# Where the second mixer's first weight pieces are loaded and converted, relative to the last down-projection stage

## The chip, the cores and the metric

The kernel runs on one core of one Trainium2 chip. The metric is the device time of one execution in microseconds (us), lower is better. Three timed executions of the kernel before took 2145.69, 2148.03 and 2148.07 us; their median, 2148.03 us, is its time. A fourth execution was taken with the hardware profiler; all rows below come from it.

## What is computed

Two residual layers of a transformer-like trunk, in float32, over 256 tokens of width 2048. Layer 0 has the "AB" mixer (neighbourhood attention beside a gated recurrence), layer 1 the "CD" mixer (pooling beside grouped-query attention). Each layer is a mixer, a layer norm, a gated feed-forward block and a second layer norm:

```
for layer in range(DEPTH):          # DEPTH = 2
    y = ab_mixer(x, ...) if layer % 2 == 0 else cd_mixer(x, ...)
    x = layer_norm(DN_ALPHA * x + y, ln_mix_g[layer], ln_mix_b[layer])
    f = swiglu(x, ffn_w_gate[layer], ffn_w_up[layer], ffn_w_down[layer])
    x = layer_norm(DN_ALPHA * x + f, ln_ffn_g[layer], ln_ffn_b[layer])

def cd_mixer(x, w_in, w_out, ...):
    proj = x @ w_in                  # 2048 x 2560, five chunks of 512 columns here
    ...
```

The place of interest is the seam between the layers: the end of layer 0's `swiglu` (its down projection), the layer norm behind it, and the first of the five column chunks of `x @ w_in` in layer 1's mixer.

## The kernel before, in words

**Tiling.** The 256 tokens are two blocks of 128, called token 0 and token 1 here (`tok` in the code). A weight matrix is read in pieces of 128 partitions x 2 x 512 float32 (512 KB). For precision every float32 operand is held as two fp32r halves, high and low, and a product is three matmuls (low x high, high x high, high x low; `mm3`, L407). So a piece goes through four steps: SyncE's queue (SP) issues its DMA into one of four buffers `raw` (L290); ScalarE (ACT) casts it to `whi` (L252); VectorE (DVE) subtracts to get `wlo` (L253); TensorE (PE) multiplies. One piece is twelve matmuls, six for each token. `load_half` does the first three steps and gives `whi` and `wlo` a slot from `rings`, some pools of buffers that are taken in turn.

**Two loop orders.** `mm_chunk` either takes a piece for both tokens and then the next piece, or (`tok_major`) loads all its pieces first, runs all of them for token 0, calls `after(0)`, and then runs all of them for token 1. The second order is used around a layer norm, so that the norm of token 0 can run while PE works on token 1.

**The seam.** The last stage of the feed-forward block (`ffn`) multiplies hidden chunks 9 and 10 with the down weights in two `mm_chunk` calls of eight pieces each: columns 0 and 1 of the output first, then columns 2 and 3 in token-major order. I number these sixteen pieces down 0 to down 15. Results lie in PSUM banks `acc` and `mx`, which ACT has seeded with the residual (L422). In `after(tok)`, DVE takes statistics of the banks (`BN_STATS` on tile `st`, L430), combines them (`BN_AGGR`, L436), adds epsilon (L356); GpSimd (POOL) takes the power for `rstd` (L359); DVE centres four columns (L445, reads the norm's gain `gam`); ACT scales them by `rstd` (L459); DVE adds the norm's bias `bet` (L460). `gam` and `bet` are loaded by two 1 MB DMAs (L497, L498).

**The flips.** A normed token then has to be transposed for the next matmuls: four groups of four transposes on PE (L249, into banks `tr` and `mx`), each evacuated by ACT (`xTh`, L486) and DVE (`xTl`, L487). They wait in the generator `pending`, and `mm_chunk` calls `step()` ahead of a piece from number `first_step` on, so that the flips of token 0 stand among the last matmuls of token 1; what is left is run at the end of the token. The constant `LATER` (7) is that number at two places: the down call for columns 2 and 3, and the first chunk of the CD mixer.

**The mixer's first chunk.** `cd_mixer` runs five chunks of eight pieces `cd_in`. Chunk 0 is token-major; its token 0 part needs only token 0's flips, and token 1's norm and flips run beside it. I call its pieces cd 0 to cd 7 and those of chunk 1 c1-0 to c1-7. Chunk 0's two result banks are evacuated by the function `kv` (`dvh`, `dvl`, squares for a norm, `rx` on L1237) before chunk 1's second token can write into the first of them, since the tag `acc` has three banks.

**What sets the order.** Instructions are put on each engine by a scheduler that simulates a timeline; `tc.high_priority` moves a group ahead, `tc.issue_after(ins)` puts what is issued inside it behind `ins`, and `tc.keep_in_program_order` pins one behind the last. Each engine then runs its own list strictly in order. Before the change the eight pieces of chunk 0 are issued by `cd_mixer`, when `ffn` has been written out; the idle y buffers (`new_yT`, three of them, and `fourth`, `y4h` and `y4l`) are set up for the CD mixer's results just before it.

Of the kernel before, what the change touches and what calls it, by code (L numbers as in the profile page):

```python
# [66 lines left out]
LATER = 7  # L67
# [141 lines left out]
def trunk(ctx: ExitStack, tc: tile.TileContext, a, out):  # L209
# [41 lines left out]
    def split(hi, lo, src):  # L251
        nc.scalar.copy(hi, src)  # L252
        return nc.vector.tensor_tensor(lo, src, hi.bitcast(F32), op=sub).ins  # L253
# [15 lines left out]
    held = [0]  # L269
    last_load = [None]  # L270
# [3 lines left out]
    def load_half(src, between=()):  # L274
        behind = ahead if held[0] > 0 else ()
        held[0] -= 1
        slots = [r for r in rings for _ in range(r[1])]
        pool, bufs = rings[0] if turn[0] < 0 else slots[turn[0] * 3 % len(slots) if len(slots) % 3 else turn[0] % len(slots)]
        turn[0] += 1
        with tc.high_priority(offset=400):  # L280
            raw = wp.tile([P, 2, NCH], F32, tag="raw", name="raw", bufs=4)
            hi = pool.tile([P, 2, NCH], F32R, tag="whi", name="whi", bufs=bufs)
            lo = pool.tile([P, 2, NCH], F32R, tag="wlo", name="wlo", bufs=bufs)
            parts = 1 + len(between)
            n = 2 // parts
            for i in range(parts):
                if i:
                    between[i - 1]()
                s = slice(i * n, (i + 1) * n)
                load = nc.sync.dma_start(raw[:, s, :], src[:, s, :])  # L290
                if first[0]:
                    tc.keep_in_program_order(load)
                last_load[0] = load.ins
                with ExitStack() as order:
                    for ins in behind:
                        order.enter_context(tc.issue_after(ins))
                    split(hi[:, s, :], lo[:, s, :], raw[:, s, :])
        return hi, lo
# [5 lines left out]
    def mm_chunk(halves, lhs, outs, tok_major=False, after=None, before=None, seeded=False, first_step=FIRST_STEP, pinned=0):  # L304

        n = len(halves)
        loaded = []
# [16 lines left out]
        if tok_major:  # L324
            for i, half in enumerate(halves):
                src = half[0]
                if pending and i >= FREE:
                    held[0] = 1
                loaded.append(load_half(src))
            for tok in range(NT):  # L330
# [6 lines left out]
                while pending:  # L337
                    step()
                if after:
                    after(tok)  # L340
# [497 lines left out]
    def ffn(layer, xT, res, mix_pool, close_mix, keep, last):  # L838
# [64 lines left out]
        def after(tok):  # L903
# [8 lines left out]
        mm_chunk(some((2, 3), [(ci, j, j) for j in (2, 3) for ci in range(2)]), yl, ends, tok_major=True, after=after, seeded=True, first_step=LATER)  # L912
        rings.pop()
        stack.close()
        return nxt
# [308 lines left out]
    def cd_mixer(mp, consts, xT, yT):  # L1224
# [102 lines left out]
        for c, (kind, _) in enumerate(cd_plan()):  # L1327
            outs = [acc() for _ in range(NT)]
            mm_chunk([(a["cd_in"][c, n], two(2 * n)) for n in range(8)], lhs, outs, tok_major=(c == 0), first_step=LATER)
            if c == 0:  # L1330
                with tc.issue_after(last_load[0]):
# [40 lines left out]
    def layer_end(i, w, groups, yT, last):  # L1372
# [11 lines left out]
        return ffn(i, xT, res, fp, close, keep, last)  # L1384

    consts = []
    xT = layer_end(0, a["ab_out"], AB_OUT_GROUPS, yT, False)
    yT = [new_yT() for _ in range(3)] + [fourth()]
    with tc.tile_pool(name="cd", bufs=1, reuse_waits="tile") as mp:
        cd_mixer(mp, consts, xT, yT)  # L1390
# [114 lines left out]
```

## Time and profile before

| | us |
|---|---|
| median of three timed runs | 2148.03 (2145.69 to 2148.07) |
| the profiled execution | 2149.07 |
| span of its instructions | 2147.3 |
| time outside the span | 1.77 |
| PE busy / DVE busy / ACT busy in the span | 2127.0 / 1763.1 / 1242.4 |
| longest idle time of PE between 10 and 2130 us | 3.35, before the matmul at 1212.69 |
| mean granted TensorE clock, whole span | 0.998 |
| granted TensorE clock, 1212.70 to 1217.20 | 0.62 |

Times of single instructions are counted from the start of the span. A row of a timeline gives start, duration, engine, line and operation with its tiles, and in brackets how long the engine had been idle and what released it. Matmuls are pipelined: one of 512 columns is shown as 0.39 us long, but the next starts 0.227 us later, so it is the distance of starts that counts. The clock column of a table of stretches is the share of full TensorE speed that was granted.

### The profile page before, as it was taken

The page shows a single profiled execution, that of the slowest core. Times are in us where ns is not written, and L with a number is a line of the kernel's source. Part 1 is how long each engine was busy: PE and PEld are TensorE (multiplying, and loading weights), DVE is VectorE, ACT ScalarE, POOL GpSimd, SP SyncE. Part 2 cuts the span into 40 slices and gives each one's busy share as a digit, 9 for nine tenths or more (in the row PEclk, how much of TensorE's full clock was granted, in tenths as well). Part 3 has the DMA queues.
Part 4 walks back from the last instruction along what each step waited for, and adds up shares of the span by engine and source line. Part 5 has one row for each costly group of instructions (what it writes and reads, how often), then busy time and mean ns, then how long its engine had stood idle before and what let it go on. Part 6 is the DMA issues. An engine that isn't in the chain of part 4 may idle for free.

```text
span 2147.3 us, 27217 instructions
## 1 busy us (share of the span) xinstructions
PE 2127.0 (99%) x9856; PEld 1771.6 (83%) x9856; DVE 1763.1 (82%) x2226; ACT 1242.4 (58%) x1618; POOL 37.5 (2%) x43
## 2 busy tenths in 40 slices
PE   8999999999999999999999999999999999999998
PEld 7888888888888888888888788888888888888886
DVE  6885688666789999999996776676999999999976
ACT  6435534555556666666676564454566666667763
POOL 0001001000000000000000000000000000000000
PEclk9999999999999999999999999999999999999999
DMA  8545545584667777767765563564777767777754
GB/s 294 168 152 185 163 157 172 181 283 144 215 250 266 253 257 257 263 237 251 264 243 191 206 233 125 183 210 157 283 255 256 257 243 248 267 247 257 255 186 176
DMA packets 118614, 477.25 MB, mean 222 GB/s; under 512 B 13904, under 2 KB 16976, under 8 KB 103376
## 3 DMA queue, kind: packets, MB, share of 16 engines
q1 hardware_dynamic: 118480, 475.53, 63.6%
q8 instruction: 77, 1.26, 0.2%
q14 instruction: 57, 0.47, 0.1%
HBM read 473.37 MB, written 2.10 MB: 221 GB/s over the span
## 4 chain that ended last, share of the span: by engine, by line
PE 97%; DVE 1%; DMA 1%; issue 0%; ACT 0%; SPq 0%; DVEq 0%; ACTq 0%
PE un L566 35%; PE acc L407 33%; PE acc L566 20%; PE mx L407 4%; PE mx L1057 1%; PE tr L249 1%; PE un L249 1%; DVE wlo L253 1%; DMA raw<-in_cd_in 1%; DMA raw<-in_down 1%; PE mx L1103 0%; PE mx L1318 0%; ACT whi L252 0%; PE mx L249 0%; DMA raw<-in_ab_in 0%
## 5 line engine op out<-in xcount | busy, mean ns | idle before, releaser
L540 ACT CAST whi<-raw 128x1024 fp32r<-128x1024 f32 x356 | 372.9, 1052 | 226.5 <-PE acc L566 72.0
L253 DVE TENSOR_TENSOR wlo<-raw,whi 128x1024 fp32r<-128x1024 f32 (+1 forms) x297 | 359.6, 1220 | 162.5 <-ACT whi L252 160.2
L544 DVE TENSOR_TENSOR wlo<-raw,whi 128x1024 fp32r<-128x1024 f32 x356 | 430.5, 1219 | 70.3 <-ACT whi L540 65.4
L252 ACT CAST whi<-raw 128x1024 fp32r<-128x1024 f32 (+1 forms) x297 | 309.3, 1049 | 298.5 <-PE acc L407 185.1
L407 PE MATMUL acc<-whi,xTl 128*128 128x512 f32 x736 | 293.3, 398 | 8.8 <-ACT whi L252 5.4
L407 PE MATMUL acc<-whi,xTh 128*128 128x512 f32 x736 | 290.9, 395 | 0.0
L407 PE MATMUL acc<-wlo,xTh 128*128 128x512 f32 x736 | 288.3, 395 | 0.0
L566 PE MATMUL acc<-whi,yTl 128*128 128x512 f32 x576 | 225.8, 392 | 0.0
L566 PE MATMUL acc<-wlo,yTh 128*128 128x512 f32 x576 | 224.4, 390 | 0.0
L566 PE MATMUL acc<-whi,yTh 128*128 128x512 f32 x576 | 224.1, 389 | 0.0
L540 ACT CAST sh<-z 128x1024 fp32r<-128x1024 f32 x108 | 113.6, 1052 | 128.6 <-DVE z L637 73.5
L566 PE MATMUL un<-whi,xTl 128*128 128x512 f32 x460 | 179.0, 389 | 0.0
L566 PE MATMUL un<-whi,xTh 128*128 128x512 f32 x460 | 178.9, 389 | 0.0
L566 PE MATMUL un<-wlo,xTh 128*128 128x512 f32 x460 | 178.9, 389 | 0.0
L407 PEld LDWEIGHTS acc<-whi,xTl 128*128 128x128 f32 x736 | 139.5, 190 | 36.7 <-ACT whi L252 6.1
L407 PEld LDWEIGHTS acc<-wlo,xTh 128*128 128x128 f32 x736 | 139.3, 189 | 28.1 <-DVE wlo L253 0.2
L407 PEld LDWEIGHTS acc<-whi,xTh 128*128 128x128 f32 x736 | 139.6, 190 | 26.7
L544 DVE TENSOR_TENSOR sl<-rs,sh 128x1024 fp32r<-128x1024 f32 x108 | 131.6, 1218 | 25.7 <-ACT sh L540 25.7
L637 DVE TENSOR_TENSOR z<-rs 128x1024 f32<-128x1024 f32 x108 | 131.6, 1219 | 3.6 <-DMA rs<-in_gu 2.9
L540 ACT CAST sh<-rs 128x1024 fp32r<-128x1024 f32 x108 | 113.6, 1052 | 34.8 <-PE un L566 27.7
L544 DVE TENSOR_TENSOR sl<-z,sh 128x1024 fp32r<-128x1024 f32 x108 | 131.5, 1217 | 0.0
L566 PEld LDWEIGHTS acc<-wlo,yTh 128*128 128x128 f32 x576 | 108.1, 188 | 22.7
(303 smaller groups left out, 3944.7 us busy)
## 6 DMA issues: line engine op xcount, KB each, us to landing
raw<-in_gu SPq DMA_DIRECT2D x244, 512.0 KB, 4.5
rs<-in_gu SPq DMA_DIRECT2D x108, 1024.0 KB, 5.0
raw<-in_down SPq DMA_DIRECT2D x176, 512.0 KB, 4.7
raw<-in_ab_in SPq DMA_DIRECT2D x127, 512.0 KB, 4.2
raw<-in_cd_in SPq DMA_DIRECT2D x40, 512.0 KB, 4.5
raw<-in_ab_out SPq DMA_DIRECT2D x32, 512.0 KB, 4.7
raw<-in_cd_out SPq DMA_DIRECT2D x32, 512.0 KB, 4.3
bias<-in_na_bias SPq DMA_DIRECT2D x32, 64.0 KB, 4.3
```

Of the source, the lines that this page charges most:

```text
L249: return nc.tensor.transpose(o, src, eye)
L252: nc.scalar.copy(hi, src)
L253: return nc.vector.tensor_tensor(lo, src, hi.bitcast(F32), op=sub).ins
L407: ins = nc.tensor.matmul(o, lhs[a], rhs[b], start=start and n == 0, stop=stop and n == 2, **more)
L540: plan.op("ACT", size, lambda: [nc.scalar.copy(high(), src())], reads, [(hi, at)])
L544: lambda: [nc.vector.tensor_tensor(low(), src(), high().bitcast(F32), op=sub)],
L566: yield nc.tensor.matmul(o.get(), x[i], r[j], start=begin and n == 0, stop=end and n == 2, **kw)
L637: lambda: [tt(g(), r()[:, 0:3:2], r()[:, 3:4].to_broadcast([P, 2, NCH]), op=add)],
L1057: nc.tensor.matmul(m[:, 2 * h + s, :], kk[:, h, s * P : (s + 1) * P], qq[:, h, r * P : (r + 1) * P], start=True, stop=True,)
```

## The change

Seven of the eight pieces of the CD mixer's chunk 0 are now issued from within the down call for columns 2 and 3, through a new hook `then` of `mm_chunk`: cd 0 to cd 4 before that call's matmuls, cd 5 and cd 6 after those of token 1. cd 3 and cd 4 get no slot of the rings but the idle y buffers (a `new_yT` pair and `fourth`), and `cd_mixer` creates its own y buffers after chunk 0. The conversions of cd 0 to cd 4 are chained one behind the other by `issue_after`, the norm of each token is put behind the last conversion issued, cd 5 behind the flips of token 0, cd 6 behind cd 5. `gam` and `bet` are still put behind the last piece loaded, which is now cd 4. The constants of the mixer are also put behind the last flip. `LATER` becomes 6. cd 7 is loaded by chunk 0 itself. No arithmetic changes.

```diff
-LATER = 7
+LATER = 6
...
     def split(hi, lo, src):
-        nc.scalar.copy(hi, src)
-        return nc.vector.tensor_tensor(lo, src, hi.bitcast(F32), op=sub).ins
+        act = nc.scalar.copy(hi, src)
+        return nc.vector.tensor_tensor(lo, src, hi.bitcast(F32), op=sub).ins, act.ins
...
-    def load_half(src, between=()):
-        behind = ahead if held[0] > 0 else ()
-        held[0] -= 1
...
+    def load_half(src, between=(), home=None, behind=None):
+        if behind is None:
+            behind = ahead if held[0] > 0 else ()
+            held[0] -= 1
...
+            if home:
+                hi, lo = (x.rearrange("p (e a) t -> p e (a t)", e=2) for x in home())
...
-                    split(hi[:, s, :], lo[:, s, :], raw[:, s, :])
+                    converted[:] = split(hi[:, s, :], lo[:, s, :], raw[:, s, :])
...
         if tok_major:
-            for i, half in enumerate(halves):
-                src = half[0]
+            for i in range(len(loaded), n):
                 if pending and i >= FREE:
                     held[0] = 1
-                loaded.append(load_half(src))
+                loaded.append(load_half(halves[i][0]))
+            if then:
+                then(0)
...
+                if then and tok == 1:
+                    then(1)
                 if after:
                     after(tok)
...
-            with tc.high_priority(offset=1000):
+            with ExitStack() as order:
+                order.enter_context(tc.high_priority(offset=1000))
                 for j in (2, 3):
                     evac(tok, j, ends[tok][j], True, True)
+                for ins in () if last else converted:
+                    order.enter_context(tc.issue_after(ins))
                 norms[0](tok, nxt, out if last else None, {j: ends[tok][j] for j in (2, 3)})
...
+        def then(tok):
+            for i in (range(5), range(5, 7))[tok]:
+                early.append(next_half(i, {3: new_yT, 4: fourth}.get(i), tuple(converted if i in (1, 2, 3, 4, 6) else ahead if i == 5 else ())))
...
-                with tc.issue_after(last_load[0]):
+                yT.extend([*(new_yT() for _ in range(3)), fourth()])
+                with tc.issue_after(last_load[0]), tc.issue_after(ahead[0]):
                     cc, sn, nw, pscale, rcount = cd_constants(consts[0])
```

In the lists below the numbers behind a name tell one buffer from another, and line numbers of the changed kernel are some 5 to 25 higher. First the DVE list around the norm of token 0, before. `raw_10309` is cd 0, `raw_10321` cd 2, `raw_10333` cd 4; `st0` on `mx_10073` is the last statistic of token 0.

```order
L253 TENSOR_TENSOR wlo_10323<-raw_10321,whi_10322 128x1024
L430 BN_STATS st0_9896<-mx_10073 128x6
L436 BN_AGGR mv_10182<-st0_9896 128x2
L356 TENSOR_SCALAR rstd_10184<-mv_10182 128x1
L445 SCALAR_TENSOR_TENSOR res0_3802<-res0_3802,mv_10182,gam_10176 128x512 x2
L445 SCALAR_TENSOR_TENSOR res0_3802<-acc_10072,mv_10182,gam_10176 128x512
L445 SCALAR_TENSOR_TENSOR res0_3802<-mx_10073,mv_10182,gam_10176 128x512
L253 TENSOR_TENSOR wlo_10311<-raw_10309,whi_10310 128x1024
L460 TENSOR_TENSOR res0_3802<-res0_3802,bet_10177 128x512
L253 TENSOR_TENSOR wlo_10335<-raw_10333,whi_10334 128x1024
L460 TENSOR_TENSOR res0_3802<-res0_3802,bet_10177 128x512 x2
```

The same place in the changed kernel, where `raw_10134`, `raw_10140`, `raw_10146` and `raw_10152` are cd 1 to cd 4:

```order
L253 TENSOR_TENSOR wlo_10136<-raw_10134,whi_10135 128x1024
L253 TENSOR_TENSOR wlo_10142<-raw_10140,whi_10141 128x1024
L253 TENSOR_TENSOR yTl_10148<-raw_10146,yTh_10147 128x1024
L438 BN_STATS st0_9896<-acc_10072 128x6
L253 TENSOR_TENSOR y4l_10154<-raw_10152,y4h_10153 128x1024
L438 BN_STATS st0_9896<-mx_10073 128x6
L444 BN_AGGR mv_10212<-st0_9896 128x2
L364 TENSOR_SCALAR rstd_10214<-mv_10212 128x1
L453 SCALAR_TENSOR_TENSOR res0_3802<-res0_3802,mv_10212,gam_10206 128x512 x2
L453 SCALAR_TENSOR_TENSOR res0_3802<-acc_10072,mv_10212,gam_10206 128x512
L453 SCALAR_TENSOR_TENSOR res0_3802<-mx_10073,mv_10212,gam_10206 128x512
L468 TENSOR_TENSOR res0_3802<-res0_3802,bet_10207 128x512 x4
```

Before, one conversion (of cd 2, out of turn) stood ahead of the last statistic and two stood among the norm's additions; now all five stand ahead, in turn, and the norm of token 0 is in one piece.

Next the DMA issues on SP's queue at the same place, before; `raw_10122` is down 15.

```order
L290 DMA raw_10122<-in_down0 128x1024
L497 DMA gam_10176<-in_ln_ffn_g 128x2048
L498 DMA bet_10177<-in_ln_ffn_b 128x2048
L290 DMA raw_10309<-in_cd_in 128x1024
L290 DMA raw_10315<-in_cd_in 128x1024
L290 DMA raw_10321<-in_cd_in 128x1024
L290 DMA raw_10327<-in_cd_in 128x1024
L290 DMA raw_10333<-in_cd_in 128x1024
```

And in the changed kernel:

```order
L295 DMA raw_10122<-in_down0 128x1024
L295 DMA raw_10128<-in_cd_in 128x1024
L295 DMA raw_10134<-in_cd_in 128x1024
L295 DMA raw_10140<-in_cd_in 128x1024
L295 DMA raw_10146<-in_cd_in 128x1024
L295 DMA raw_10152<-in_cd_in 128x1024
L505 DMA gam_10206<-in_ln_ffn_g 128x2048
L506 DMA bet_10207<-in_ln_ffn_b 128x2048
L295 DMA raw_10305<-in_cd_in 128x1024
L295 DMA raw_10311<-in_cd_in 128x1024
L295 DMA raw_10343<-in_cd_in 128x1024
```

`gam` and `bet` moved behind five pieces; before they stood ahead of all of them.

Last, DVE's list where token 1's flips end and chunk 0's first bank is evacuated, before. `raw_10541`, `raw_10559`, `raw_10577`, `raw_10595` and `raw_10613` are c1-0 to c1-4.

```order
L487 TENSOR_TENSOR xTl1_9895<-tr_10399,xTh1_9893 128x512
L253 TENSOR_TENSOR dvl_10495<-acc_10307,dvh_10494 128x256
L487 TENSOR_TENSOR xTl1_9895<-mx_10412,xTh1_9893 128x512
L487 TENSOR_TENSOR xTl1_9895<-tr_10419,xTh1_9893 128x512
L487 TENSOR_TENSOR xTl1_9895<-mx_10426,xTh1_9893 128x512
L358 TENSOR_SCALAR rstd_10503<-ss_10499 128x2
L253 TENSOR_TENSOR wlo_10543<-raw_10541,whi_10542 128x1024
L1237 SCALAR_TENSOR_TENSOR rx_10506<-acc_10307,rstd_10503,nwk_10487 128x128 x2
```

And in the changed kernel:

```order
L495 TENSOR_TENSOR xTl1_9895<-mx_10418,xTh1_9893 128x512
L1233 TENSOR_SCALAR nwq_10485<-nwq_10485 128x128
L253 TENSOR_TENSOR wlo_10543<-raw_10541,whi_10542 128x1024
L253 TENSOR_TENSOR wlo_10579<-raw_10577,whi_10578 128x1024
L253 TENSOR_TENSOR wlo_10597<-raw_10595,whi_10596 128x1024
L253 TENSOR_TENSOR wlo_10561<-raw_10559,whi_10560 128x1024
L253 TENSOR_TENSOR dvl_10495<-acc_10341,dvh_10494 128x256
L253 TENSOR_TENSOR wlo_10615<-raw_10613,whi_10614 128x1024
L366 TENSOR_SCALAR rstd_10503<-ss_10499 128x2
L1262 SCALAR_TENSOR_TENSOR rx_10506<-acc_10341,rstd_10503,nwk_10487 128x128 x2
```

Five conversions of chunk 1 now stand between the last flip and the evacuation, where one stood before. On PE only the places of the flips move: the first flip group of each token stands one piece (six matmuls) earlier, the second too. Some instructions of the CD mixer's later stages (pooling, attention and the output projection) also change places by a few rows, on PE, ACT and DVE.

More of the change, by code (lines that the diff above doesn't have):

```diff
@@ L301, in two, with mm_chunk @@
         return k, k + 1
-    def mm_chunk(halves, lhs, outs, tok_major=False, after=None, before=None, seeded=False, first_step=FIRST_STEP, pinned=0):
+    def mm_chunk(halves, lhs, outs, tok_major=False, after=None, before=None, seeded=False, first_step=FIRST_STEP, pinned=0, loaded=(), then=None):
         n = len(halves)
-        loaded = []
+        loaded = list(loaded)
         def step():
@@ L836, in inner, with ffn @@
         return groups, [lambda g=g, y=y, t=t: transpose4(g(), *(e[:, :, t * P : (t + 1) * P] for e in y.get()), 1000) for g, _, y, t in flips]
-    def ffn(layer, xT, res, mix_pool, close_mix, keep, last):
+    def ffn(layer, xT, res, mix_pool, close_mix, keep, last, next_half=None):
         lhs = x_lhs(xT)
@@ L906, in after @@
                     norms.append(residual_tools(res, *load_gb(fp, layer, "ffn"), stats)[2])
-            with tc.high_priority(offset=1000):
+            with ExitStack() as order:
+                order.enter_context(tc.high_priority(offset=1000))
                 for j in (2, 3):
                     evac(tok, j, ends[tok][j], True, True)
+                for ins in () if last else converted:
+                    order.enter_context(tc.issue_after(ins))
                 norms[0](tok, nxt, out if last else None, {j: ends[tok][j] for j in (2, 3)})
-        mm_chunk(some((2, 3), [(ci, j, j) for j in (2, 3) for ci in range(2)]), yl, ends, tok_major=True, after=after, seeded=True, first_step=LATER)
+        def then(tok):
+            for i in (range(5), range(5, 7))[tok]:
+                early.append(next_half(i, {3: new_yT, 4: fourth}.get(i), tuple(converted if i in (1, 2, 3, 4, 6) else ahead if i == 5 else ())))
+        early = []
+        mm_chunk(
+            some((2, 3), [(ci, j, j) for j in (2, 3) for ci in range(2)]),
+            yl,
+            ends,
+            tok_major=True,
+            after=after,
+            seeded=True,
+            first_step=LATER,
+            then=None if last else then,
+        )
         rings.pop()
         stack.close()
-        return nxt
+        return nxt, early
     def attend(pool, probs, v_of):
@@ L1222, in cd_bands, with cd_mixer @@
         return band
-    def cd_mixer(mp, consts, xT, yT):
+    def cd_mixer(mp, consts, xT, yT, early):
         lhs = x_lhs(xT)
@@ L1328, in cd_mixer @@
             outs = [acc() for _ in range(NT)]
-            mm_chunk([(a["cd_in"][c, n], two(2 * n)) for n in range(8)], lhs, outs, tok_major=(c == 0), first_step=LATER)
+            mm_chunk([(a["cd_in"][c, n], two(2 * n)) for n in range(8)], lhs, outs, tok_major=(c == 0), first_step=LATER, loaded=early if c == 0 else ())
             if c == 0:
-                with tc.issue_after(last_load[0]):
+                yT.extend([*(new_yT() for _ in range(3)), fourth()])
+                with tc.issue_after(last_load[0]), tc.issue_after(ahead[0]):
                     cc, sn, nw, pscale, rcount = cd_constants(consts[0])
@@ L1383, in layer_end @@
         xT = out_proj(w, groups, yT, res, load_gb(fp, i, "mix"))
-        return ffn(i, xT, res, fp, close, keep, last)
+        return ffn(i, xT, res, fp, close, keep, last, lambda n, home, behind: load_half(a["cd_in"][0, n], (), home, behind))
     consts = []
-    xT = layer_end(0, a["ab_out"], AB_OUT_GROUPS, yT, False)
-    yT = [new_yT() for _ in range(3)] + [fourth()]
+    xT, early = layer_end(0, a["ab_out"], AB_OUT_GROUPS, yT, False)
+    yT = []
     with tc.tile_pool(name="cd", bufs=1, reuse_waits="tile") as mp:
-        cd_mixer(mp, consts, xT, yT)
+        cd_mixer(mp, consts, xT, yT, early)
     layer_end(1, a["cd_out"], CD_OUT_GROUPS, yT, True)
```

12 lines of the change are left out of this document (7 added, 5 removed).

## The prediction

> **What bounds the kernel now.** I read the page first: busy times, then the chain that ended last.
>
> ```profile
> span 2147.3 us, 27217 instructions
> PE 2127.0 (99%) x9856; PEld 1771.6 (83%) x9856; DVE 1763.1 (82%) x2226; ACT 1242.4 (58%) x1618; POOL 37.5 (2%) x43
> PE 97%; DVE 1%; DMA 1%; issue 0%; ACT 0%; SPq 0%; DVEq 0%; ACTq 0%
> ```
>
> PE does 99% of the span, and the change removes no matmul. So it can win only where PE is idle or slow. A table of stretches around the seam between the layers shows where (columns: length, busy us of PE, weight loads, DVE, ACT, POOL, granted clock, DMA share, GB/s).
>
> ```profile
> 1185.00:1190.00 5.00, 5.00 (x23) 4.13 (x22) 3.16 (x5) 1.57 (x3) 0.00 (x0) 1.00 0.95 393
> 1195.00:1200.00 5.00, 5.00 (x24) 4.14 (x23) 1.61 (x2) 2.01 (x2) 0.00 (x0) 1.00 0.06 24
> 1200.00:1210.00 10.00, 8.53 (x44) 6.52 (x42) 9.93 (x16) 7.04 (x9) 0.99 (x1) 1.00 0.44 157
> 1210.00:1230.00 20.00, 17.31 (x77) 14.31 (x78) 16.36 (x27) 10.23 (x20) 1.69 (x2) 0.91 0.52 180
> 1230.00:1260.00 30.00, 30.00 (x136) 24.75 (x135) 22.04 (x30) 18.68 (x27) 0.70 (x1) 1.00 0.80 272
> ```
>
> PE is full up to 1200 and from 1230 on; between them it lacks 1.47 + 2.69 us and runs 20 us at a clock of 0.91. PE's timeline shows each loss.
>
> ```profile
> 1195.23 0.39 PE L407 MATMUL acc<-whi,yTl 128*128 128x512 f32 x1
> 1204.52 0.39 PE L407 MATMUL mx<-wlo,yTh 128*128 128x512 f32 x1
> 1205.23 0.63 PE L249 MATMUL tr<-ident,res 128*128 128x128 f32 x4 [0.33 <-DVE res L460]
> 1208.68 0.66 PE L249 MATMUL mx<-ident,res 128*128 128x128 f32 x4 [0.48 <-DVE res L460]
> 1212.69 0.50 PE L407 MATMUL acc<-whi,xTl 128*128 128x512 f32 x1 [3.35 <-DVE xTl L487]
> 1213.88 0.63 PE L407 MATMUL acc<-whi,xTh 128*128 128x512 f32 x1
> 1216.43 0.63 PE L407 MATMUL acc<-whi,xTh 128*128 128x512 f32 x1
> 1223.96 0.60 PE L249 MATMUL tr<-ident,res 128*128 128x128 f32 x4
> 1227.02 0.48 PE L407 MATMUL acc<-whi,xTl 128*128 128x512 f32 x1
> ```
>
> Token 1 of the down stage starts at 1195.23; 42 matmuls later (1204.52 is the 42nd) the distance is (1204.52 - 1195.23)/41 = 0.2266 us. Then PE waits three times for token 0's norm and flips, 4.16 us in all, and after the 3.35 us the matmuls from 1213.88 to 1216.43 come 0.425 apart (six distances): a halved clock for some 3.4 us, 8 matmuls, 1.6 us.
>
> Why is the norm late? DVE's list and the ACT row that it hangs on:
>
> ```profile
> 1188.10 1.23 DVE L253 TENSOR_TENSOR wlo<-raw,whi 128x1024 fp32r<-128x1024 f32 x1 [1.84 <-ACT whi L252]
> 1197.31 2.01 ACT L252 CAST whi<-raw 128x1024 fp32r<-128x1024 f32 x2 [5.65 <-DMA raw<-in_cd_in]
> 1198.39 1.23 DVE L253 TENSOR_TENSOR wlo<-raw,whi 128x1024 fp32r<-128x1024 f32 x1 [7.26 <-ACT whi L252]
> 1199.54 0.69 DVE L430 BATCH_NORM_STATS2 st<-mx 128x6 f32<-128x512 f32 x1
> 1200.63 1.41 DVE L445 SCALAR_TENSOR_TENSOR res<-res,mv,gam 128x512 f32<-128x512 f32 x2
> 1203.27 1.22 DVE L253 TENSOR_TENSOR wlo<-raw,whi 128x1024 fp32r<-128x1024 f32 x1
> 1204.40 0.68 DVE L460 TENSOR_TENSOR res<-res,bet 128x512 f32<-128x512 f32 x1
> ```
>
> Token 0's last matmul ends about 1195.4, but DVE, in order, sits idle 7.26 us in front of cd 2's conversion, which waits for cd 2's transfer; the last statistic comes 4.1 us late, and two more conversions stand in the norm. The transfers are late because they were issued behind `gam` and `bet`:
>
> ```profile
> 1176.70 3.88 SPq L290 DMA_DIRECT2D raw<-in_down  x3
> 1180.63 0.42 SPq L497 DMA_DIRECT2D gam<-in_ln_ffn_g  x1
> 1181.11 0.42 SPq L498 DMA_DIRECT2D bet<-in_ln_ffn_b  x1
> 1182.60 17.37 SPq L290 DMA_DIRECT2D raw<-in_cd_in  x5
> DMA to landing us min/median/max: 8.7/8.7/8.7
> DMA to landing us min/median/max: 12.4/12.4/12.4
> DMA to landing us min/median/max: 10.9/10.9/10.9
> DMA to landing us min/median/max: 9.1/9.1/9.1
> DMA to landing us min/median/max: 3.1/4.6/6.7
> ```
>
> The last five are from the answers on `gam`, `bet`, cd 2, cd 3 and the sixteen down pieces: these land after 4.6 us (6.7 for down 15, issued last before `gam`), cd 2 needed 10.9 and cd 3 9.1. At 1185 to 1190 the DMA engines are 95% busy, at 1195 to 1200 only 6%: the burst of 2 MB of norm constants is what delays the pieces.
>
> **The change part by part.** *Ceiling.* From 1195.23 plus 36 matmuls (1203.4) to token 1's first matmul of chunk 0 (1227.02) PE has 60 matmuls and eight flip groups. Sixty at 0.2268 are 13.6 us. One token's flips with six matmuls take 1227.02 - 1223.96 = 3.06, less six matmuls 1.70, twice 3.4. Without any wait chunk 0's token 1 would start at 1203.4 + 17.0 = 1220.4: **6.6 us** earlier. That is the 4.16 of waits, 1.6 of slow clock, and some 0.8 of broken-up flip groups.
>
> *Early pieces.* The first SP row at 1182.60 is cd 0's issue, set by a free `raw` buffer, so it is the same in the changed kernel, now with no norm constants ahead of it. At 4.6 us it lands at 1187.2; cast 1.05 and subtraction 1.23 end at about 1189.5, right behind down 15's (which ended 1189.3, and is earlier now). DVE and ACT idle here, so five conversions (5 x 1.22 on DVE) cost PE nothing: they fill the 7.26 us gap. cd 4 needs cd 0's `raw`, and on SP `gam` and `bet` queue behind that wait: issued about 1189.5, 1189.9 and 1190.4.
>
> *Norm of token 0.* A wait is added: the norm stands behind cd 4's conversion on both engines. Behind it on ACT are the four scalings and the flips' casts, on DVE the last statistic and everything after. From cd 4's landing: cast 1.1, subtraction 1.2, statistic 0.6, combine and `rstd` to the first centring 0.5, four centrings 2.64 (1200.63 to 1203.27), first addition 0.7: 6.7 us to the first flip. cd 4's latency was not measured with `gam` and `bet` right behind it; nearest is down 15 with 6.7, issued 0.4 us ahead of them (the third issue of the first SP row). Bounds are 3.1 and, from cd 2, 10.9; I take 6.7 as the nearest case: landing 1196.2, first flip ready 1202.9. PE wants it at 1203.4 (piece 6, because of `LATER` 6), the second 1.8 later; the additions come every 0.6. So no wait, with 0.5 us to spare; at 4.6 us there are 2.6.
>
> *`bet` behind five pieces.* Its landing after 12.4 us gives 1202.8, and the first addition ends 1203.5: a wait of 0.1. Bounds are 6.7 (down 15 under the same load: no wait) and 12.4 plus one more piece ahead, 0.524 MB at 393 GB/s or 1.3 us: 13.7, a wait of 1.4.
>
> [...]
>
> *Token 1.* cd 5 and cd 6 are converted between token 0's flips and token 1's norm, cd 7 behind the norm. Rows of token 1 before:
>
> ```profile
> 1217.62 0.15 DVE L356 TENSOR_SCALAR rstd<-mv 128x1 f32<-128x1 f32 x1
> 1220.33 2.49 DVE L460 TENSOR_TENSOR res<-res,bet 128x512 f32<-128x512 f32 x4
> 1222.73 1.22 DVE L253 TENSOR_TENSOR wlo<-raw,whi 128x1024 fp32r<-128x1024 f32 x1
> 1230.69 0.60 DVE L1237 SCALAR_TENSOR_TENSOR rx<-acc,rstd,nwk 128x128 f32<-128x128 f32 x2
> ```
>
> Token 0's last two flip groups now start at 1207.0 and 1207.4, chunk 0 at 1207.9. The last `xTl` ends near 1209.5, two conversions take DVE to 1212.1, `rstd` is at 1212.4; as in the rows, the first addition ends 3.4 later (1215.8) and cd 7's conversion 6.3 later (1218.7). PE wants the flip at 1216.0 and cd 7's `wlo` at 1218.7. Both are just in time; I charge 0.3.
>
> *Other edits at nothing.* The constants issued early are wanted after 1220; a y buffer as a weight slot is read like any other; the pinned order of the layer's end in layer 1 is untouched. The later stages change places by a few rows only, with PE full there (30.00 of 30.00); I take 0, bounds -0.5 to +1.
>
> *Sum.* 6.6 - 0.3 = **6.3 us**. The profiled execution takes 2147.3 + 1.77 = 2149.07, the changed one 2142.8. The median of the runs is 1.04 below the profiled execution, so the median forecast is 2148.03 - 6.3 = **2141.7**.
>
> **The rivals.**
>
> *The wait only changes its piece (18%).* The norm still waits for a transfer, cd 4's in place of cd 2's. With cd 3's 9.1 us, cd 4 lands at 1198.6 and the first flip is ready at 1205.3, 1.9 us late; the later flips are hidden by that. Gain 4.4, or 2143.6. With cd 2's 10.9 it is 3.7 late, long enough for the slow stretch of 1.6 to come back: gain 1.0, or 2147.0. For it: the two transfers stand right behind cd 4. [...]
>
> *Chunk 1 waits for a bank (12%).* Five conversions of chunk 1, one of them (c1-4) behind a fresh transfer, now stand ahead of the evacuation whose last row was at 1230.69. c1-0 is converted near 1223.8, c1-4 is issued then, lands 3.1 later, cast, squares, `rstd` and `rx` follow: about 1231.2 (3.1) to 1232.5 (4.6). Chunk 1's token 1 wants the bank at 1220.7 + 10.9 + 1.4 = 1233.0. At 6.7 us it is 1.7 late: 2143.4. For it: before there were 8 us to spare, now 1. Against: lonely transfers take 3.1.
>
> *`bet` lands far too late (6%).* This is slower than before. If packets of `gam` and `bet` are served behind all pieces in flight, PE's first flip waits from a landing of 1202.7 on, microsecond for microsecond, and from 3.35 us of waiting the slow stretch adds its 1.6. It eats the gain at a landing of 1207.4, 17 us after issue. At 20 us (1210.4): 7.7 + 1.6 - 6.3, 3 us slower, 2151. Against it: 12.4 was the longest seen with the engines 95% busy.
>
> [...]
>
> *The later stages lose what was won (4%).* A few rows reordered between 1290 and 1400 make new waits of 3 us: 2144.7. Nothing in the table shows one.
>
> **How the numbers follow.** The forecast has 60%: 2141.7, with its own range 2141.4 (all 6.6) to 2142.9. The three runs before spread 2.4 us, so I give the low end 2139.6. The high end takes in the bank rival, the late stages and the better half of the first rival, up to 2145.8; beyond are the slow cases (6) and the rest of the first rival (9), and with 3 below that is less than 2 in 10. About 0.2% (4.3 us, times below 2143.7) is what a measurement can tell from no change. Faster by more: the forecast nearly whole (56), a third of the first rival (6), half of the second (6): 0.68. Within: the rest of these and of the late stages, 0.26. Slower: 0.06.
>
> **What would show it.** In the changed profile: no PE idle time above 0.5 us and a clock of 1.00 between 1200 and 1230; the conversion of cd 0 on DVE near 1188 and no DVE idle time above 3 us before the last statistic of token 0; that statistic at 1197 to 1199; `bet` landing before 1203; chunk 0's token 1 starting at 1220 to 1221; chunk 1 without a wait for `rx`. A DVE wait for `y4h` beyond 1199, a flip released by `bet`'s landing, or a wait at chunk 1's seventh matmul would each make the number wrong, by the prices above.

## The result and the profile after

| | before | after |
|---|---|---|
| median of eleven timed runs, same chip, us | 2145.95 (2145.09 to 2148.07) | 2142.16 (2141.75 to 2142.69) |
| ratio after to before | | 0.9981 (95% interval 0.9973 to 0.9989) |
| profiled execution / its span, us | 2149.07 / 2147.3 | 2142.16 / 2140.4 |
| PE waits between 1200 and 1230 us | 4.16 | none |
| spread of the eleven runs | 3.0 | 0.9 |

The changed kernel is faster by 3.8 us (0.18%). The forecast of 2141.7 is 0.5 us below the median, but it was reached from a median of before of 2148.03, and eleven runs put that at 2145.95: the gain forecast was 6.3, the gain measured 3.8. That gap is the main question below.

The page of the changed kernel, first lines and the chain by engine:

```profile
span 2140.4 us, 27211 instructions
PE 2124.7 (99%) x9856; PEld 1770.1 (83%) x9856; DVE 1765.2 (82%) x2226; ACT 1243.6 (58%) x1618; POOL 40.7 (2%) x43
PE 99%; DVE 0%; DMA 0%; SPq 0%; issue 0%; ACT 0%
```

PE's chain went from 97 to 99% of the span. The table of stretches around the seam (columns as in the prediction):

```profile
1185.00:1190.00 5.00, 5.00 (x24) 4.14 (x23) 4.68 (x5) 3.31 (x5) 0.00 (x0) 1.00 0.85 304
1195.00:1200.00 5.00, 5.00 (x24) 4.14 (x23) 4.72 (x9) 1.95 (x4) 0.55 (x1) 1.00 0.99 412
1200.00:1210.00 10.00, 10.00 (x54) 8.35 (x53) 7.33 (x11) 4.84 (x8) 0.00 (x0) 1.00 0.47 177
1210.00:1230.00 20.00, 20.00 (x98) 16.61 (x97) 17.11 (x27) 11.40 (x19) 1.70 (x2) 1.00 0.51 164
```

PE is full throughout at a clock of 1.00; DVE works 4.72 of the 5 us from 1195 on, where it worked 1.61; and the DMA engines are 99% busy there, where they were at 6%: the norm's constants now travel beside the conversions. PE's timeline at the first flip and at chunk 0's token 1:

```profile
1202.42 0.39 PE L415 MATMUL mx<-wlo,yTh 128*128 128x512 f32 x1
1202.65 0.60 PE L249 MATMUL tr<-ident,res 128*128 128x128 f32 x4
...
1219.84 0.47 PE L415 MATMUL acc<-whi,xTl 128*128 128x512 f32 x1
```

No row has a bracket, so nothing was waited for. This trace runs 0.74 us ahead of that of before when it reaches the seam (the 5600th matmul starts at 1200.38 and at 1201.12); in before's count the first flip stands at 1203.4 and token 1 starts at 1220.6. DVE's list in the same stretch:

```profile
1187.10 1.23 DVE L253 TENSOR_TENSOR wlo<-raw,whi 128x1024 fp32r<-128x1024 f32 x1 [0.32 <-ACT whi L252]
...
1194.69 1.21 DVE L253 TENSOR_TENSOR y4l<-raw,y4h 128x1024 fp32r<-128x1024 f32 x1
1195.82 0.69 DVE L438 BATCH_NORM_STATS2 st<-mx 128x6 f32<-128x512 f32 x1
...
1197.20 1.42 DVE L453 SCALAR_TENSOR_TENSOR res<-res,mv,gam 128x512 f32<-128x512 f32 x2 [0.21 <-DMA gam<-in_ln_ffn_g]
...
1199.86 2.48 DVE L468 TENSOR_TENSOR res<-res,bet 128x512 f32<-128x512 f32 x4
...
1211.56 0.15 DVE L364 TENSOR_SCALAR rstd<-mv 128x1 f32<-128x1 f32 x1
...
1216.68 1.22 DVE L253 TENSOR_TENSOR wlo<-raw,whi 128x1024 fp32r<-128x1024 f32 x1
...
1229.71 0.61 DVE L1262 SCALAR_TENSOR_TENSOR rx<-acc,rstd,nwk 128x128 f32<-128x128 f32 x2 [0.82 <-POOL rstd L367]
```

The statistic behind cd 4's conversion (`y4l`) came at 1195.82, not 1199.54, and the additions stand in one piece. From that statistic on, the only wait of token 0's norm for a transfer is 0.21 us for `gam`. Landings by tile, `bet`'s and, in a window around its issue, cd 4's:

```profile
L506 SPq DMA_DIRECT2D bet<-in_ln_ffn_b x1: 424/424/424, 1190.1 to 1190.1; - x1
DMA to landing us min/median/max: 9.6/9.6/9.6
L295 SPq DMA_DIRECT2D raw<-in_cd_in x1: 328/328/328, 1188.4 to 1188.4; - x1
DMA to landing us min/median/max: 4.7/4.7/4.7
```

### The profile page after: what moved, and what is told of

Read it like the earlier page. It is cut to its first block, busy times and chain, and to the rows that moved or that the text cites. A ratio compares the mean times of both kernels' runs of the same rounds, so it can differ in the third digit from the quotient of the medians.

```text
span 2140.4 us, 27211 instructions
## 1 busy us (share of the span) xinstructions
PE 2124.7 (99%) x9856; PEld 1770.1 (83%) x9856; DVE 1765.2 (82%) x2226; ACT 1243.6 (58%) x1618; POOL 40.7 (2%) x43
## 4 chain that ended last, share of the span: by engine, by line
PE 99%; DVE 0%; DMA 0%; SPq 0%; issue 0%; ACT 0%
PE un L574 35%; PE acc L415 34%; PE acc L574 20%; PE mx L415 5%; PE mx L1082 1%; PE tr L249 1%; PE un L249 1%; PE mx L1128 0%; PE mx L1343 0%; PE mx L249 0%; DMA raw<-in_ab_in 0%; PE mx L1326 0%; DVE res L457 0%; DVE res L453 0%; SPq L986 0%
## 5 line engine op out<-in xcount | busy, mean ns | idle before, releaser
L253 DVE TENSOR_TENSOR wlo<-raw,whi 128x1024 fp32r<-128x1024 f32 (+1 forms) x295 | 358.3, 1225 | 153.8 <-ACT whi L252 151.2
```

## A measure for the seam

Every kernel here runs 9856 matmul rows on PE. Call **seam time** the distance from the start of the 5600th to that of the 5800th (counted from 0), read from the trace; the change lies between them. It splits the difference of the two spans (2147.29 - 2140.36 = 6.93 us): start to the 20th matmul 0.56, from there to the 5600th 0.18, **seam 48.03 - 41.59 = 6.44**, from the 5800th to the last matmul -0.23, the tail behind it 0. So between the two *profiled* executions the seam gave 6.44, close to the 6.3 forecast. The timed runs gave 3.8. The experiments ask why, and what each part of the change is worth.

All profiles, with the waits of PE in the seam that are over 0.08 us, seam time, and what seam time has above the changed kernel's 41.59 beside those waits:

| kernel | PE waits, us | seam time | rest | profiled us | median us |
|---|---|---|---|---|---|
| before | 0.33, 0.48, 3.35 | 48.03 | 2.28 | 2149.07 | 2145.95 |
| e1 before, again | 3.35 | 46.79 | 1.85 | 2148.31 | 2147.44 |
| e6 before, third | 1.98, 0.30, 0.85 | 45.44 | 0.72 | 2145.93 | |
| e12 before, fourth | 3.35 | 46.92 | 1.98 | 2148.91 | |
| e8 LATER 6 alone | 2.22 | 44.07 | 0.26 | 2144.63 | 2146.43 |
| e3 constants early | 2.06 | 43.85 | 0.20 | 2145.13 | 2147.02 |
| e2 order alone | 1.23 | 43.02 | 0.20 | 2144.19 | 2144.45 |
| e7 without the order | 1.10 | 42.89 | 0.20 | 2144.30 | 2143.36 |
| e4 constants first | 0.64 | 42.39 | 0.16 | 2142.88 | 2144.15 |
| e11 LATER 7 | 0.20 | 41.99 | 0.20 | 2146.30 | 2143.18 |
| after | none | 41.59 | | 2142.16 | 2142.16 |
| e5 after, again | none | 41.57 | | 2141.89 | 2142.03 |
| e9 three `bet` | 11.11 | 54.91 | 2.21 | 2157.41 | 2157.03 |
| e10 five `bet` | 20.41 | 63.55 | 1.55 | 2164.11 | 2165.72 |

e1 to e4 shared a chip (the kernel before there 2147.19, 33 runs), e5 to e8 another (2146.44, 27 runs), e9 to e12 a third (2146.72, 15 runs); ratios are to those.

## The experiments

**The two kernels unchanged: e1, e6, e12 (before) and e5 (after).** No edit.

> The kernel before, unchanged. Theory: its eleven runs fall in two groups (2145.1 to 2146.2 and 2147.7 to 2148.1) because the 3.35 us wait ahead of chunk 0 lowers the clock in some executions only. Then the runs fall in the same two groups; if the profiled execution is below 2146.5, its matmuls behind the wait stand 0.227 us apart with a clock of 1.00 and the waits still sum to about 4.2 us; if it is above 2147.5, some 8 matmuls stand 0.425 apart. Rival: the groups differ at the start of the program or in another wait; then the slow matmuls are there in either group.

> The kernel before, a third profile. Two profiles of it show the 200 matmuls around the seam (the 5600th to the 5800th) in 48.0 and 46.8 us, the changed kernel 41.6. Theory A, the long wait ahead of chunk 0 is always there (it hangs on DVE's list, which is fixed) and only the slow stretch behind it comes and goes: a wait of 3 us or more ahead of chunk 0's first matmul, and 44.5 to 48 us for those matmuls, nearer to 45 where the clock stays at 1.00. Theory B, the wait hangs on how soon the norm constants and cd 2 land and varies itself: a wait below 2.5 us in a third profile, with cd 2's latency below 10 us.

> The kernel before, a fourth profile. In three profiles of it cd 2 landed 3.89, 5.14 and 6.54 us ahead of the 5600th matmul, and the 200 matmuls from there took 48.03, 46.79 and 45.44 us: their sum is 51.92, 51.93 and 51.98. Theory A, cd 2's landing alone sets the seam: the sum is 51.7 to 52.2 again, whatever the landing is. Theory B, the agreement of three is chance (two of them have the slow stretch and no late conversion of cd 7, one has it the other way): the sum is off by 0.5 us or more.

> The changed kernel once more, unedited. Its eleven runs lay within 0.9 us of each other (2141.75 to 2142.69), those of the kernel before within 3 us there and within 6.7 us on the chip of the last comparison (2144.11 to 2150.78). Theory A, the waits in the seam make the kernel before vary from run to run: here too the changed kernel's runs lie within 1.5 us of each other, at 2141.5 to 2143, and the kernel before beside them is 3 to 5 us slower and spreads by 2.5 us or more. Theory B, the chip of the last comparison is noisier for any kernel: the spread of the changed kernel is like that of the kernel before, 3 us or more on a noisy chip. In its profile both expect no wait of PE above 0.3 us between 1200 and 1230.

e1 gave 2147.44 us (ratio 1.0002, 0.9993 to 1.0011). Its theory of two groups of runs did not hold: its eleven lie between 2145.36 and 2149.26 us, none further than 0.9 from the next. The slow stretch itself does come and go: it stands in the profiled executions of before, e1 and e12 (2149.07, 2148.31 and 2148.91 us) and not in that of e6 (2145.93). PE's waits in chunk 0 in e1, e6 and e12, one fence each:

```profile
1211.58 0.50 PE L407 MATMUL acc<-whi,xTl 128*128 128x512 f32 x1 [3.35 <-DVE xTl L487]
```

```profile
1209.08 0.50 PE L407 MATMUL acc<-whi,xTl 128*128 128x512 f32 x1 [1.98 <-DVE xTl L487]
1219.63 0.50 PE L407 MATMUL acc<-whi,xTl 128*128 128x512 f32 x1 [0.30 <-ACT whi L252]
1221.22 0.50 PE L407 MATMUL acc<-wlo,xTh 128*128 128x512 f32 x1 [0.85 <-DVE wlo L253]
```

```profile
1212.10 0.50 PE L407 MATMUL acc<-whi,xTl 128*128 128x512 f32 x1 [3.35 <-DVE xTl L487]
```

And ACT's cast of cd 2 on which DVE's list hangs, in e6 and in e12 (in the prediction it is the row at 1197.31):

```profile
1193.70 1.05 ACT L252 CAST whi<-raw 128x1024 fp32r<-128x1024 f32 x1 [4.59 <-DMA raw<-in_cd_in]
```

```profile
1196.72 2.00 ACT L252 CAST whi<-raw 128x1024 fp32r<-128x1024 f32 x2 [5.43 <-DMA raw<-in_cd_in]
```

And what stands ahead of token 1's `rstd` on DVE, in e6:

```profile
1214.69 0.23 DVE L1208 TENSOR_SCALAR nwq<-nwq 128x128 f32<-128x128 f32 x1 [1.97 <-DMA nwq<-in_d_q_norm]
```

By the trace cd 2 landed 3.89, 5.14, 6.54 and 4.99 us ahead of the 5600th matmul (before, e1, e6, e12; issue to landing 10.94, 10.47, 8.79 and 10.64 us), and seam time was 48.03, 46.79, 45.44 and 46.92. The sums are 51.92, 51.93, 51.98 and 51.91, as e12's theory A expected. The rows show less than that theory, though.

Up to chunk 0 one landing sets the time: chunk 0's first matmul starts 15.46 us behind cd 2's landing in all four, and in e8 too, whose norm stands in the same order. That landing differs between executions by 2.65 us; the profiled execution behind the prediction had the latest of the four.

From chunk 0's first matmul to the 5800th the landing does not set the time: 36.46 us in the three with the slow stretch, 36.52 in e6 without it, 34.88 in e8 and 34.87 in the changed kernel. In e6, 1.15 us of waiting for cd 7's late cast and conversion take the place of the slow stretch, and these stand behind token 1's norm, whose `rstd` was held on DVE by another transfer: the mixer's constant `nwq` (1.97 us; 1.15 in before, 1.88 in e1, 1.48 in e12). That the two losses have one size is chance as far as these profiles show, and e8, with neither, has a sum of 50.34. So theory B of e6 holds: the wait itself varies (1.98 and 3.35) with cd 2's latency. But the whole seam does not follow from that one landing.

In the changed kernel PE waits for no transfer in the seam. The `nwq` wait is gone too (the row stands behind the last flip, at 1221.51), but no run here moves the mixer's constants alone, so what that edit is worth is not shown. e5 gave 2142.03 beside 2146.44 us, ratio 0.9978 (0.9970 to 0.9987). Its eleven runs spread over 1.8 us (ten of them within 0.9), a little more than theory A said; the 27 runs of the kernel before spread over 5.1.

**e2: the order alone.** The kernel before with chunk 0's conversions put behind token 0's norm; loads, constants and `LATER` as before.

```diff
-        behind = ahead if held[0] > 0 else ()
+        behind = ahead if held[0] > 0 else norm0 if left0[0] > 0 else ()
         held[0] -= 1
+        left0[0] -= 1
...
+            if tok == 0:
+                norm0[:] = ahead
...
+            if c == 0:
+                left0[0] = 8
```

> The kernel before, with only the order changed: chunk 0's conversions are put behind token 0's norm; no piece is loaded early, norm constants stay ahead of the pieces, LATER stays 7. Theory A (the loss comes from the conversion that stands ahead of the last statistic): the statistic runs at about 1195.5, the first flip is in time, and the four conversions behind it end before chunk 0 wants them at 1207.9; PE waits below 1.5 us, time 2142.2 to 2143.7. Rival B (the pieces have to be converted early): PE waits for chunk 0's weights instead, 2144.5 or more.

2144.45 us, ratio 0.9988 (0.9979 to 0.9996). No wait at token 0; one moved to token 1:

```profile
1218.99 0.50 PE L410 MATMUL acc<-wlo,xTh 128*128 128x512 f32 x1 [1.23 <-DVE wlo L253]
```

The conversions are late now and not the norm, so chunk 0's last piece (cd 7) is what PE waits for. Neither range was hit: the wait is below theory A's 1.5 us, but it is for weights, as rival B said, and the median lies between the two. The order alone brings 2.7 us, more than half of the gain, though cd 2 took 8.77 us as in e6.

**e3: the constants early, alone.** `gam` and `bet` issued ahead of the last down pieces; nothing else.

```diff
+        gb = None if last else load_gb(fp, layer, "ffn")
...
+        if not last:
+            norms.append(residual_tools(res, *gb, stats)[2])
...
-            if tok == 0:
+            if tok == 0 and last:
```

> The kernel before, with only the two norm constants loaded earlier, ahead of the last down pieces. The scheduler then puts two conversions (cd 2 and cd 4) ahead of the last statistic. Theory A (what counts is that the statistic stands behind a fresh transfer): cd 4 is issued when cd 2 is converted, about 1193, lands about 1197, the statistic comes at 1199 to 1200 as before, gain 0 to 1.5 us, 2144.5 to 2146. Rival C (the burst of norm constants is the cause): the pieces land early and 3 us or more are won, 2143 or less.

2147.02 us, ratio 1.0002 (0.9994 to 1.0011): nothing. cd 2 now took 4.2 us and landed at 1190.5, but the wait only moved to another piece. ACT and DVE at the place:

```profile
1190.59 1.05 ACT L252 CAST whi<-raw 128x1024 fp32r<-128x1024 f32 x1 [0.38 <-DMA raw<-in_cd_in]
1196.12 2.00 ACT L252 CAST whi<-raw 128x1024 fp32r<-128x1024 f32 x2 [4.48 <-DMA raw<-in_cd_in]
```

```profile
1197.20 1.23 DVE L253 TENSOR_TENSOR wlo<-raw,whi 128x1024 fp32r<-128x1024 f32 x1 [3.70 <-ACT whi L252]
1198.35 0.69 DVE L430 BATCH_NORM_STATS2 st<-mx 128x6 f32<-128x512 f32 x1
```

cd 4, whose buffer is free only at 1192.9, stands ahead of the last statistic in this list. (Its profiled execution was the fastest of its eleven, so its seam time of 43.85 is not that of a usual run.)

**e4: the changed kernel with the constants ahead of cd 0 to cd 4.**

```diff
+        def norm_constants():
+            with tc.issue_after(last_load[0]):
+                norms.append(residual_tools(res, *load_gb(fp, layer, "ffn"), stats)[2])
+
         def after(tok):
-            if tok == 0:
-                with tc.issue_after(last_load[0]):
-                    norms.append(residual_tools(res, *load_gb(fp, layer, "ffn"), stats)[2])
+            if tok == 0 and last:
+                norm_constants()
...
         def then(tok):
+            if tok == 0:
+                norm_constants()
             for i in (range(5), range(5, 7))[tok]:
```

> The changed kernel, with the two norm constants issued ahead of cd 0 to cd 4 again. Theory: the pieces land as late as before (1194.8 to 1198.5 in the time of the kernel before), cd 4 about 1200, the norm behind it starts near 1202.6 and the first flip is ready near 1206.4, 3 us after PE wants it: 2145.2, or 2146.8 if the clock drops. Rival (the order on DVE and ACT is what won, the order of the transfers does not matter): 2142.2.

2144.15 us (2142.23 to 2148.0), ratio 0.9986 (0.9977 to 0.9995). cd 4's cast and the first flip:

```profile
1197.10 1.05 ACT L252 CAST y4h<-raw 128x1024 fp32r<-128x1024 f32 x1 [0.94 <-DMA raw<-in_cd_in]
```

```profile
1203.15 0.52 PE L249 MATMUL tr<-ident,res 128*128 128x128 f32 x3 [0.64 <-DVE res L468]
```

With the 2 MB of `gam` and `bet` back ahead of the pieces, cd 0 lands only at 1191.31 and cd 4 at 1197.07 (1185.94 and 1193.06 in the changed kernel); DVE works through the conversions from 1192.47 on, the norm stands behind them, and the first flip waits 0.64 us, where 3 were expected. Seam time is 0.80 above the changed kernel's, so in the trace the place of `gam` and `bet` is part of the gain, once the order is there. The medians do not settle it: the changed kernel was not run on this chip, and the interval of the ratio overlaps its own. Nor do the runs show where their spread of 5.8 us comes from; e1's eleven on the same chip spread over 3.9.

**e7: the changed kernel without the order.** No chain between the conversions, no norm behind them, cd 5 and cd 6 free.

```diff
-                for ins in () if last else converted:
+                for ins in ():
...
-                early.append(next_half(i, {3: new_yT, 4: fourth}.get(i), tuple(converted if i in (1, 2, 3, 4, 6) else ahead if i == 5 else ())))
+                early.append(next_half(i, {3: new_yT, 4: fourth}.get(i), ()))
```

> The changed kernel without the order: no chain from conversion to conversion, and the norm isn't put behind them; the early issue, the idle y buffers and LATER 6 stay. Theory A, the order is needed too: the scheduler lets a conversion or two slip among the norm's additions as before (1.2 us each), the first flip waits 0.7 to 2.5 us, and the median is 1 to 2.5 us above the changed kernel's. Theory B, the early issue is what counts: no wait above 0.5 us in the seam and a median within 0.5 us of the changed kernel's.

2143.36 us, ratio 0.9985 (0.9976 to 0.9994): 3.1 us below the kernel before and 1.3 above the changed kernel on the same chip. DVE's and PE's rows:

```profile
1202.79 1.23 DVE L253 TENSOR_TENSOR wlo<-raw,whi 128x1024 fp32r<-128x1024 f32 x1 [1.37 <-ACT whi L252]
1203.93 1.29 DVE L468 TENSOR_TENSOR res<-res,bet 128x512 f32<-128x512 f32 x2
```

```profile
1204.77 0.41 PE L249 MATMUL tr<-ident,res 128*128 128x128 f32 x2 [1.10 <-DVE res L468]
```

cd 5, which lands at 1201.6 behind the constants, slips between centring and additions; DVE waits 1.37 us for it and PE 1.10. Theory A. So the early issue without the order already wins 3.1 us (e7), and the order without the early issue 2.7 (e2): what they win is in large part the same by these medians, and only both together leave no wait.

**e8: `LATER` 6 alone, and e11: the changed kernel with `LATER` 7.**

```diff
-LATER = 7   # e8; e11 has the reverse
+LATER = 6
```

> The kernel before with LATER 6 alone, so that the flips of token 0 stand one piece (six matmuls) earlier. Theory A, the long wait is DVE's work being late and a wait of 3.35 us brings the slow clock: the sum of the waits ahead of chunk 0 stays at 4 to 5.5 us but is split between the flips and chunk 0's first matmul, the largest below 3 us, the clock stays at 1.00 between 1200 and 1230, and the time is 0.5 to 1.6 us below that of the kernel before. Theory B, the clock falls for another reason: a stretch at 0.8 or 0.9 appears all the same, and the time is within 0.5 us of the kernel before or above it.

> The changed kernel with LATER back at 7: the first flips of each token stand six matmuls (1.36 us) later. Theory A, LATER is not what gains, since the first flip is ready 2 us ahead of its place in the changed kernel: no wait of PE above 0.3 us in the seam, median within 0.4 us of the changed kernel's 2142.0 to 2142.2. Theory B, the flips then stand too near to chunk 0's first matmul, which waits for their evacuation: 0.5 us or more of waiting there, and as much in the median.

e8: 2146.43 us, ratio 1.0000 (0.9991 to 1.0009). Its profiled execution was again its fastest, with one wait (2.22 us) and the clock at 1.00 behind it:

```profile
1209.66 0.49 PE L407 MATMUL acc<-whi,xTl 128*128 128x512 f32 x1 [2.22 <-DVE xTl L487]
```

The waits were not split between the flips and chunk 0, as was expected, and the median shows no gain; what its slower runs wait for was not profiled. e11: 2143.18 us, ratio 0.9984 (0.9975 to 0.9993), whose interval overlaps e5's; seam time is 0.4 above the changed kernel's, with a wait of 0.20 for cd 7. The wait is as theory A said, the median is not: 1.0 to 1.2 us above the changed kernel's on other chips, where 0.4 was the most expected. (Its profiled execution, 2146.30, is an outlier of its eleven: it lost 3.9 us in a later stage, which the last section shows.) `LATER` is worth 0.4 us by the profile, about 1 by medians from different chips: not settled closer.

**e9 and e10: `bet` loaded three and five times.**

```diff
-        nc.sync.dma_start(b, a[f"ln_{which}_b"][i : i + 1, :].to_broadcast([P, D]))
+        [nc.sync.dma_start(b, a[f"ln_{which}_b"][i : i + 1, :].to_broadcast([P, D])) for _ in range(3 if (which, i) == ("ffn", 0) else 1)]
```

> The changed kernel with the DMA of bet issued three times, one behind the other, into the same buffer with the same data. It doubles the suspected cost of bet behind five pieces. In two profiles of the changed kernel bet lands 2.5 us behind gam, so the third bet should land 5.0 us later than the one does now, at 1204.6 in the time base of the first profile; the first addition ends 0.7 later, and the first flip, which stands at 1202.65 there, waits 2.6 us. Theory A, a wait in the seam costs itself, and below 3 us leaves the clock alone: the 5600th to the 5800th matmul take 41.6 + 2.6 to 3.6 us (up to 1 more from cd 5 to cd 7 landing late too), clock 1.00, median 2144.5 to 2145.7. Theory B, later waits hide it or packets of bet run beside those of the pieces: less than 1 us more, below 2143.

> The same with five DMAs of bet: the last lands 10 us later, at 1209.6, and the first flip waits 7.6 us. Theory A, a wait above 3 us also brings the halved clock for 1.6 us: the 200 matmuls take 41.6 + 7.6 + 1.6 = 50.8 us or a little more, the clock falls below 1.00 behind the wait, and the median is 2151 to 2153, slower than the kernel before. Theory B, no slow stretch: 49.2 us and 2149.6.

2157.03 us, ratio 1.0044 (1.0032 to 1.0057), and 2165.72, ratio 1.0090 (1.0077 to 1.0104): far slower than either theory said. The loads did not queue back to back: each later one, writing the same buffer, was issued only when the one before had landed (the second 3.8 us behind that landing, with other loads ahead of it in SP's list, the others at once). e9's loads by tile, and its first flips:

```profile
L506 SPq DMA_DIRECT2D bet<-in_ln_ffn_b x3: 328/328/422, 1191.5 to 1210.4; - x3
DMA to landing us min/median/max: 4.7/6.0/9.1
```

```profile
1215.99 1.09 PE L249 MATMUL tr<-ident,res 128*128 128x128 f32 x4 [11.11 <-DVE res L468]
...
1218.15 0.63 PE L415 MATMUL mx<-whi,yTl 128*128 128x512 f32 x1
1218.58 0.63 PE L415 MATMUL mx<-whi,yTh 128*128 128x512 f32 x1
...
1220.56 0.39 PE L415 MATMUL mx<-whi,yTh 128*128 128x512 f32 x1
1220.79 0.40 PE L415 MATMUL mx<-wlo,yTh 128*128 128x512 f32 x1
```

The third was issued at 1210.4 and landed at 1215.05; the flip follows 0.94 us behind, and after the 11.11 us the matmuls come 0.43 us apart before they return to 0.23. e10's fifth was issued at 1217.7:

```profile
1223.26 1.09 PE L249 MATMUL tr<-ident,res 128*128 128x128 f32 x4 [20.41 <-DVE res L468]
```

The size expected was wrong, since it took the loads as one stream. The price holds: seam time rose by 13.32 and 21.96 us for waits of 11.11 and 20.41, the wait itself and 1.6 to 2.2 more.

## Why the prediction was right, and where it was wrong

*Ceiling 6.6 and sum 6.3.* Right as working on the profile it started from: seam time fell by 6.44. The 4.16 of waits and the slow clock (1.7 by the last section, 1.6 taken) were both there and both went.

*"The median of the runs is 1.04 below the profiled execution, so the median forecast is 2148.03 - 6.3."* **This step failed.** It treats the loss in the seam as a constant of the kernel. e1, e6 and e12 show that its wait follows cd 2's landing, that the slow stretch is not always there, and that seam time ranges over 2.6 us; the profiled execution had the longest of four. Eleven runs have a median of 2145.95, and if all else is as in the profiled execution of the changed kernel, that leaves a seam of 41.59 + 3.79 = 45.4 us (an estimate): e6's 45.44, a wait of 2 us without the slow stretch. So the term over-sized is the median run's share of the waits and of the 1.6: 6.3 was taken, 3.8 to 4.4 was there (two chips). None of the rivals has the kernel before vary. That the time itself came out near 2141.7 is luck: two errors offset each other, a base that three runs put 2.1 too high and a gain that was 2.5 too large. The 0.68 for a gain above 4.3 us rests on the same step; 3.8 came, for which 0.26 was left.

*Early pieces hidden.* Right: five conversions stand in what was DVE's idle time, no idle time before the last statistic is over 0.95 us, and PE stays full.

*Norm of token 0, cd 4's latency taken at 6.7.* Over-sized: it took 4.7, and 5.8 in e5. The first addition starts at 1199.86 and takes some 0.6, the flip stands at 1202.65: 2.2 us to spare, not 0.5. By these rows a norm some 2 us later would still cost nothing (an estimate), which fits the small spread of the runs; no run tests it.

*`bet` behind five pieces at 12.4.* Over-sized too: 9.6, and 9.8 in e5. It landed at 1199.68, or 1200.4 in before's count, behind cd 4 (1193.06) and `gam` (1197.18) and ahead of cd 5 (1200.93): in the order of issue, and no wait came of it.

*Token 1, charged 0.3.* There was no wait. `rstd` came at 1211.56 and cd 7's conversion, started at 1216.68, ended at about 1217.9 (1212.3 and 1218.6 in before's count), each 0.1 us ahead of what was worked out.

*The rivals.* "The wait only changes its piece" did not happen here, but it is what e3 does for cd 4, e7 for cd 5, and e4 in part for cd 0 to cd 4: it is the early issue and the order together that exclude it. The bank: `rx` came at 1229.71, or 1230.4 in before's count, ahead of the 1231.2 to 1232.5 worked out, since c1-4 landed 3.4 us behind its issue; chunk 1 has no wait. "`bet` far too late" has the price it was given (e9, e10): the flip follows the landing by 0.95 us, so that it waits from a landing of 1202.4 on in before's count, where 1202.7 was said. Later stages: -0.23 us from the 5800th matmul on, within what two profiles of one kernel differ by there (887.2 to 887.6).

## What to carry to other kernels

A profile is one execution: where a wait hangs on a transfer, profile the kernel two or three times and see how far that landing moves before a median is forecast from its waits. DVE took its list in order in these profiles (in that of before it sat idle 7.26 us in front of cd 2's conversion), so an early load helps only as far as no late one stands ahead in the list of what waits: early constants won nothing (e3), where cd 4 still stood ahead of the last statistic. The order without early pieces won 2.7 us (e2), early pieces without the order 3.1 (e7), both 3.8 to 4.4; parts that overlap in this way cannot be added up. The changed kernel, which has time to spare behind its last transfer, also spreads less between runs: 1.8 us in eleven beside 5.1 in 27 on one chip, 0.9 beside 3.0 in eleven each on another.

## What was not expected of the hardware

The same two loads of 1 MB, issued at the same place behind the same work, landed 2.6 us apart in e6 (`gam` to `bet`) and 4.0 to 4.2 us apart in the other three profiles of the kernel before; in the changed kernel it was 2.5 twice. cd 2 landed 3.5 to 3.9 us behind `bet` in all four, so this is more than half of the 2.65 us by which its landing moves. Why is open.

In the seam the slow clock came behind every idle time of PE of 3.35 us or more and behind none of 2.22 or less. The five with it are before, e1 and e12 (a clock of 0.85, 0.76 and 0.75 from 1210 to 1215), e9 (0.50 from 1215 to 1220) and e10 (0.50 from 1220 to 1225); in e8, with 2.22, it is 1.00 throughout the seam. The loss does not grow with the wait: seam time beyond the waits is 1.85 to 2.28 us for 3.35, 2.21 for 11.11 and 1.55 for 20.41, of which 0.2 to 0.7 is there with short waits too. Nor does the length of a wait decide alone. In e11's outlier, in a stage that no edit here touches, two short waits with one group of transposes between them had the same effect:

```profile
1716.95 0.63 PE L249 MATMUL un<-ident,g 128*128 128x128 f32 x4 [1.24 <-ACT whi L548]
1718.15 0.63 PE L249 MATMUL un<-ident,g 128*128 128x128 f32 x4 [0.57 <-DVE g L686]
```

The matmuls behind them come 0.42 to 0.43 us apart from 1719.09 to 1722.49 and 0.23 to 0.24 apart from there on. The clock column around the slow stretch, in before and in e11 (columns as in the prediction):

```profile
1210.11:1213.52 3.41, 0.83 (x4) 0.70 (x5) 3.41 (x5) 2.51 (x4) 0.00 (x0) 1.00 0.71 239
1213.53:1216.93 3.40, 3.40 (x10) 2.63 (x9) 2.80 (x5) 0.00 (x0) 0.00 (x0) 0.50 0.82 260
```

```profile
1715.00:1720.00 5.00, 3.18 (x17) 2.26 (x16) 5.00 (x6) 3.91 (x6) 0.00 (x0) 0.91 0.36 120
1720.00:1725.00 5.00, 5.00 (x18) 3.99 (x17) 2.46 (x4) 1.05 (x1) 0.00 (x0) 0.75 0.65 211
```

In before the clock falls only 0.84 us after PE has started again, at 1212.69. The loss is half of the slow time that PE still has ahead of it: 1.7 us in before, where all 3.4 us of it were left. In e9 the clock is at 0.50 from 1215 to 1220 and at 0.96 in the 5 us behind, so half clock lasts to about 1220.4, 4.4 us after the flip at 1215.99; in e10 the 0.74 from 1222 to 1230 takes it to about 1226.2, 2.9 us after the flip at 1223.26. Half of these is 2.2 and 1.5 (estimates from the clock columns), beside the 2.21 and 1.55 above.

What makes the clock fall, and how much idle time that takes, these profiles do not show. One wait of 3.35 us had it behind it in all three profiles that have one, a wait of 2.22 in e8 and the 1.98 in e6 did not, and e11's 1.24 and 0.57, 1.81 us in all, did. So "below 3 us leaves the clock alone", as theory A of e9 has it, does not hold for e11's waits.
